# Low parts of sixteen gate weight blocks, worked out two stages early and kept in DRAM

## The chip, the core and the metric

The kernel runs on one core of one Trainium2 chip. What counts is the device time of one execution in microseconds (us), here the median of three.

## The reference

The reference is two transformer parts in a row on one sequence of 256 tokens with 1024 channels, all in float32. The first has two layers, sparse and dilated attention, each with a gated feed-forward. The second is a feed-forward at half weight, a mixer of three branches with gates, and another feed-forward. Cut to what the change touches:

```python
def swiglu(h, w_up, w_down):
    a, b = jnp.split(h @ w_up, 2, axis=-1)
    return (jax.nn.silu(a) * b) @ w_down
...
x = x + 0.5 * swiglu_ffn(rms_norm(x, ffn1_norm[l]), ffn1_w_in[l], ffn1_w_out[l])
h = rms_norm(x, mix_norm[l])
q_a, k_a, v_a, q_i, k_i, w_i, u_s, q_m, gates = jnp.split(h @ w_in[l], offsets, axis=-1)
...
g = jax.nn.sigmoid(gates.reshape(b_, s_, N_BRANCHES, D_MODEL))
merged = g[:, :, 0] * o_a + g[:, :, 1] * o_b + g[:, :, 2] * o_m
x = x + merged @ w_out[l]
x = x + 0.5 * swiglu_ffn(rms_norm(x, ffn2_norm[l]), ffn2_w_in[l], ffn2_w_out[l])
```

Here `o_a` is an attention over the 64 best keys of an index score, `o_b` a state space layer (S5) with a gated output, `o_m` an attention over 256 memory tokens. `w_in` of the mixer has 4548 columns; the last 3072 are the gates.

## The kernel before

The stages run in order: nsa (sparse attention), ffn0, dil (dilated attention), ffn1, ffn1_2, mix (mixer), ffn2_2 and the final norm. "First, second and third feed-forward" below are ffn0, ffn1 and ffn1_2. Activations lie transposed, as eight tiles of 128 channels x 256 tokens.

To keep float32 precision each operand is split into a high part that the fast matmul format holds exactly and a low part, the rest. A product is three matmuls (`mm3`, L230 to L232): high by high, low by high and high by low. Activations are split once per norm (xh, xl). Weights come as 1 MB loads `raw` on SP's DMA queue (`load`, L180; four buffers) of two blocks of 1024 rows x 128 columns. `split` makes from each block a high part wh, a copy on ScalarE (L189), and a low part wl = raw - wh, a subtraction on VectorE (L190); of wh and of wl there are four buffers each. A block then feeds 24 matmuls.

A feed-forward (`ffn`) starts with a norm: squares on ScalarE, their sum sqacc on GpSimd (L295) and TensorE (L301), then rv, rr and the factor R, copied by VectorE in two halves (L332). Products with the un-normed activations run meanwhile; each product is multiplied by R afterwards (fa, fb, L408 and L410), so the first such product needs R. `between` puts work of the second part into the loop: in ffn1 the norm of the memory tokens, in ffn1_2 the memory keys (`mem_keys`) and the S5 preparation (`s5_prepare`, with a pool `s5pre` of its own): a few hundred small operations on VectorE and GpSimd (constants s5..., rotation factors CS, a block matrix Z), whose results go to DRAM (rot_scratch, bt_scratch) and are read in the mixer as CSr and BT.

A list scheduler places the instructions by a cost model of its own: it may move work of a later stage to an earlier place where dependences and buffers allow, and each engine then runs its list in that order. Buffers are shared by address: a pool opened later can take the space of one that is closed, and then waits until that is free. `ffn1` holds a pool `hid` for its 22 pairs of hidden tiles. In the mixer, `gate(j)` makes the gates in column order; those with j > 1 are the branches S5 and memory (lists G1 and G2), sixteen blocks.

Of the kernel before, what the change touches and what calls it, by code (L numbers as in the profile page):

```python
# [11 lines left out]
F32 = mybir.dt.float32  # L12
F32R = mybir.dt.float32r
AF = mybir.ActivationFunctionType
ALU = mybir.AluOpType
# [3 lines left out]
P = 128  # L19
S = 256  # L20
D = 1024
KD = D // P
FF = 2816
# [99 lines left out]
class Builder:  # L123
# [84 lines left out]
    def ahead(self, units):  # L208

        first = next(units)  # L210
        return itertools.chain([first], units)

    def wide_units(self, w, K, c0, cols):

        res = []
        n = 1024 // cols
        for k0 in range(0, K // P, 2 * n):
            kb = min(2 * n, K // P - k0)
            v = self.load(w, k0 * P, kb, c0, cols)
            for k in range(0, kb, n):  # L220
                m = min(n, kb - k)
                res += self.split(v[:, k:k + m, :], m, cols)
        return res
# [161 lines left out]
        return X, R  # L385


    def ffn(self, xs, gain, w_up, w_down, factor, between=None, after=None, skew=0):
        nc, tc = self.nc, self.tc
        with tc.tile_pool(name=self.n("hid"), bufs=1) as hp:  # L390
            if skew:
                self.pad(hp, skew)
            if after:
                X, R = self.norm_twice(hp, xs, after, gain)
            else:
                (X,), R, _ = self.norm_all(xs, [gain])
            H = []
            for mp in range(KF // 2):
                if mp == 2 and between:
                    between()  # L400
                ua = self.units(w_up, D, mp * 256)
                ub = self.units(w_up, D, FF + mp * 256)
                for c in range(2):
                    k = 2 * mp + c
                    pa = self.proj(next(ua), X)
                    pb = self.proj(next(ub), X)
                    a = hp.tile([P, S], F32, tag="fa", name=self.n("fa"), bufs=2)
                    nc.vector.tensor_tensor(a, pa, R, ALU.mult)  # L408
                    b = hp.tile([P, S], F32, tag="fb", name=self.n("fb"), bufs=2)
                    nc.vector.tensor_tensor(b, pb, R, ALU.mult)  # L410
                    nc.scalar.activation(a, a, AF.Silu)
                    nc.vector.tensor_tensor(b, a, b, ALU.mult)
                    h = hp.tile([P, S], F32R, name=self.n("hh"), tag=f"hh{k}")
                    l = hp.tile([P, S], F32R, name=self.n("hl"), tag=f"hl{k}")
                    nc.scalar.activation(h, b, AF.Copy)
                    nc.vector.tensor_tensor(l, b, h.bitcast(F32), ALU.subtract)
                    H.append((h, l))
            self.out_proj(xs, w_down, FF, H, factor)

    def out_proj(self, xs, w, K, X, factor):  # L420
        nc = self.nc
        for mp in range(4):
            for c, u in enumerate(self.units(w, K, mp * 256)):
                ps = self.proj(u, X)
                m = 2 * mp + c
                nc.vector.scalar_tensor_tensor(xs[m], ps, float(factor), xs[m], ALU.mult, ALU.add)
# [66 lines left out]
    def key_parts(self, pool, ps, R, dst):  # L493
# [5 lines left out]
        for gp in range(2):  # L499
            h, o = slice(64 * gp, 64 * gp + 64), slice(64 - 64 * gp, 128 - 64 * gp)  # L500
            H, L = dst(gp)
            nc.scalar.activation(H[h], t[h], AF.Copy)
            nc.vector.tensor_tensor(L[h], t[h], H[h].bitcast(F32), ALU.subtract)
            nc.scalar.activation(H[o], t[h], AF.Copy)
# [616 lines left out]
    def mixer(self, xs):  # L1121
        nc, tc, A = self.nc, self.tc, self.A
        V, G = nc.vector, nc.gpsimd
        w = A["w_in_2"]
        (X,), R, _ = self.norm_all(xs, ["mix_norm_2"])
        with ExitStack() as es:
            mp = es.enter_context(tc.tile_pool(name="mix", bufs=1))
# [66 lines left out]

            def gate(j):
                for c in range(2 * j, 2 * j + 2):
                    for u in self.units(w, D, 1476 + c * 256):
                        gt = mp.tile([P, S], F32, name=self.n("sg"), tag="sg", bufs=24)
                        V.tensor_tensor(gt, self.proj(u, X), R, ALU.mult)
                        nc.scalar.activation(gt, gt, AF.Tanh, scale=0.5)  # L1200
                        yield gt
# [6 lines left out]
            for p in range(2):  # L1208
# [22 lines left out]
                for kb in range(2):  # L1231
                    for i, pt in enumerate(pts):
                        h = 2 * p + i
# [84 lines left out]
def body(tc, A, out, stages=None):  # L1318
    stages = stages or STAGES
    with ExitStack() as ctx:  # L1320
        b = Builder(ctx, tc, A)
        nc = b.nc
        xs, first = [], []
# [7 lines left out]
        if "nsa" not in stages:  # L1331
            b.bias_rows()
        late = None
        for s in stages:
            if s in ("ffn1", "fin1", "ffn1_2", "mix") and late is None:
                late = ctx.enter_context(tc.tile_pool(name="late", bufs=1))
            if s == "nsa":
                b.nsa(xs, first)
            elif s == "ffn0":
                b.ffn(xs, "norm_ffn0", A["ffn_w_up0"], A["ffn_w_down0"], 1.0)  # L1340
            elif s == "dil":
                b.dilated(xs)
            elif s == "ffn1":
                b.ffn(xs, "norm_ffn1", A["ffn_w_up1"], A["ffn_w_down1"], 1.0, lambda: b.mem_norm(late), skew=352)
                b.mem_project(late)
            elif s == "fin1" and "ffn1_2" not in stages:
                b.final(xs, "final_norm")
# [98 lines left out]
```

## Time and profile before

| | us |
|---|---|
| median of three executions | 1339.74 |
| the three | 1345.21, 1339.74, 1337.02 |
| the profiled execution | 1342.72 |
| its span | 1340.9 |
| TensorE busy | 1316.3 |
| VectorE busy | 1001.4 |
| ScalarE busy | 748.1 |
| GpSimd busy | 193.3 |

The profiled execution is a single one with a profile; its span is the time from its first to its last instruction. Its granted TensorE clock was 0.988 on average. A matmul is shown longer than the distance to the next (a pipeline), so a stretch in which TensorE is idle, or in which its clock is under 1.00, tells more than its busy time. PE, DVE, ACT, POOL and SP in rows are TensorE, VectorE, ScalarE, GpSimd and SyncE.

### The profile page before, as it was taken

To read this page: it belongs to the slowest core of one execution; us is meant where nothing else is said; L and a number is where in the kernel's file an instruction comes from. 1 tells how busy PE (TensorE), PEld (TensorE's weight loads), DVE (VectorE), ACT (ScalarE), POOL (GpSimd) and SP (SyncE) were. 2 spreads that over 40 slices of the span, in tenths; PEclk is the share of its full clock that TensorE was granted. 3 is DMA by queue.
4 is the path that set the end of the run, shared out by engine and by line. 5 is a ranking of instruction groups with operands and counts; after the bars stand their busy time and mean duration, and the time that the engine had idled before them with its cause. 6 is when DMAs were issued, how large, how long until landed. Compare 5 with 4: busy or idle time off the path is not lost.

```text
span 1340.9 us, 27511 instructions
## 1 busy us (share of the span) xinstructions
PE 1316.3 (98%) x10944; PEld 1250.6 (93%) x10944; DVE 1001.4 (75%) x2108; ACT 748.1 (56%) x1414; POOL 193.3 (14%) x236
## 2 busy tenths in 40 slices
PE   8999999999999999999999999999999999999997
PEld 8887899999999887899999999999987879999997
DVE  7899677766797663999965877766689887777743
ACT  5678555555668776654544555544434665555442
POOL 3300100001310000433100310001032044100011
PEclk8999999999999999989999999999999999999999
DMA  9742266646766340466656465655754254566561
GB/s 290 240 157 78 81 206 198 199 152 201 240 214 184 105 142 9 142 197 220 220 185 210 153 208 191 197 194 174 251 165 137 79 186 151 177 198 199 163 197 49
DMA packets 227120, 232.77 MB, mean 174 GB/s; under 512 B 5944, under 2 KB 221184, under 8 KB 226992
## 3 DMA queue, kind: packets, MB, share of 16 engines
q1 hardware_dynamic: 223392, 226.14, 53.2%
q10 hardware_dynamic: 3600, 4.88, 1.1%
q8 instruction: 86, 1.41, 0.4%
q14 instruction: 42, 0.34, 0.1%
HBM read 226.69 MB, written 4.30 MB: 172 GB/s over the span
## 4 chain that ended last, share of the span: by engine, by line
PE 56%; DVE 4%; issue 1%; ACT 1%; DMA 1%; POOL 1%; DVEq 0%; POOLq 0%; ACTq 0%
PE mm L230 7%; PE mm L231 7%; PE mm L232 7%; PE tr L232 4%; PE tr L230 4%; PE tr L231 4%; PE sc L230 4%; PE sc L231 4%; PE sc L232 4%; PE ov L230 2%; PE ov L231 2%; PE ov L232 2%; PE ov L488 1%; DVE wl L190 1%; PE sc L792 1%
## 5 line engine op out<-in xcount | busy, mean ns | idle before, releaser
L189 ACT ACTIVATE wh<-raw 128x1024 fp32r<-128x1024 f32 (+2 forms) x405 | 419.0, 1039 | 437.8 <-PE mm L231 135.4
L190 DVE TENSOR_TENSOR wl<-raw,wh 128x1024 fp32r<-128x1024 f32 (+2 forms) x405 | 490.9, 1214 | 162.6 <-ACT wh L189 157.1
L230 PE MATMUL mm<-xh,wh 128*128 128x256 f32 x952 | 272.9, 287 | 1.4 <-ACT wh L189 1.4
L231 PE MATMUL mm<-xl,wh 128*128 128x256 f32 x952 | 269.4, 283 | 0.0
L232 PE MATMUL mm<-xh,wl 128*128 128x256 f32 x952 | 269.0, 283 | 0.2 <-DVE wl L190 0.2
L230 PEld LDWEIGHTS mm<-xh,wh 128*128 128x128 f32 x952 | 181.8, 191 | 7.8 <-issue 4.7
L231 PEld LDWEIGHTS mm<-xl,wh 128*128 128x128 f32 x952 | 182.0, 191 | 3.9 <-issue 3.7
L232 PEld LDWEIGHTS mm<-xh,wl 128*128 128x128 f32 x952 | 181.3, 190 | 2.4 <-issue 1.5
L295 POOL TENSOR_TENSOR sqacc<-sqacc,sq 128x256 f32<-128x256 f32 x60 | 64.0, 1068 | 597.0 <-ACT sq L294 326.4
L230 PE MATMUL sc<-xh,wh 128*128 128x256 f32 x464 | 128.5, 277 | 0.0
L232 PE MATMUL sc<-xh,wl 128*128 128x256 f32 x464 | 128.5, 277 | 0.0
L231 PE MATMUL sc<-xl,wh 128*128 128x256 f32 x464 | 128.3, 277 | 0.0
L230 PE MATMUL tr<-xh,wh 128*128 128x256 f32 x440 | 123.4, 280 | 0.8 <-DVE u L446 0.8
L231 PE MATMUL tr<-xl,wh 128*128 128x256 f32 x440 | 123.2, 280 | 0.0
L232 PE MATMUL tr<-xh,wl 128*128 128x256 f32 x440 | 123.0, 280 | 0.0
L231 PEld LDWEIGHTS sc<-xl,wh 128*128 128x128 f32 x464 | 87.2, 188 | 0.0
L230 PEld LDWEIGHTS sc<-xh,wh 128*128 128x128 f32 x464 | 87.2, 188 | 0.0
L232 PEld LDWEIGHTS sc<-xh,wl 128*128 128x128 f32 x464 | 87.1, 188 | 0.0
L230 PEld LDWEIGHTS tr<-xh,wh 128*128 128x128 f32 x440 | 83.9, 191 | 1.1 <-DVE u L446 1.1
L231 PEld LDWEIGHTS tr<-xl,wh 128*128 128x128 f32 x440 | 84.1, 191 | 0.0
L232 PEld LDWEIGHTS tr<-xh,wl 128*128 128x128 f32 x440 | 84.0, 191 | 0.0
L230 PE MATMUL ov<-xh,wh 128*128 128x256 f32 x224 | 62.2, 278 | 0.0
(475 smaller groups left out, 3396.0 us busy)
## 6 DMA issues: line engine op xcount, KB each, us to landing
raw<-in_ffn_w_up_dram SPq DMA_DIRECT2D x44, 1024.0 KB, 5.4
raw<-in_ffn_w_in_dram SPq DMA_DIRECT2D x44, 1024.0 KB, 5.3
raw<-in_w_in_dram SPq DMA_DIRECT2D x17, 1024.0 KB, 5.3
raw<-in_ffn_w_down_dram SPq DMA_DIRECT2D x16, 1024.0 KB, 5.3
raw<-in_ffn_w_out_dram SPq DMA_DIRECT2D x16, 1024.0 KB, 5.2
raw<-in_b_w_q_dram SPq DMA_DIRECT2D x12, 1024.0 KB, 5.2
raw<-in_a_w_in_dram SPq DMA_DIRECT2D x8, 1024.0 KB, 9.2
bt<-u_scratch SPq DMA_DIRECT2D x28, 256.0 KB, 4.3
```

The lines of the kernel that those rows point to most:

```text
L189: nc.scalar.activation(hv, v, AF.Copy)
L190: nc.vector.tensor_tensor(lv, v, hv.bitcast(F32), ALU.subtract)
L230: nc.tensor.matmul(ps, sh, mh, start=(i == 0), stop=False)
L231: nc.tensor.matmul(ps, sh, ml, start=False, stop=False)
L232: nc.tensor.matmul(ps, sl, mh, start=False, stop=(i == n - 1))
L295: nc.gpsimd.tensor_tensor(acc[:, 0], acc[:, 0], s, ALU.add)
L488: nc.tensor.matmul(O[64 * i:64 * i + 64, q0:q1], V[kb], pt[:, c0:c0 + q1 - q0], start=(start and kb == 0), stop=(stop and kb == 1), skip_g ...
L792: nc.tensor.matmul(ps, Q[d, h][:, qb * P:qb * P + P], K[d][g], start=(i == 0), stop=(i == 1))
```

## The change

Sixteen blocks of the mixer's `w_in`, those of the gates with j > 1, get their low parts in ffn0 and ffn1. `low_parts` is a generator; each step loads one block (512 KB, lraw) on SP's queue, copies the high part (lh) on ScalarE, subtracts on VectorE (ll) and stores the result on ScalarE's DMA queue to a DRAM tensor low_scratch. `ffn` takes a step in every odd round of its up-projection and `out_proj` one in each of its four rounds: nine in ffn0, seven in ffn1. Its tiles (two lraw, one lh, two ll, 4 KB per partition each, 20 KB in all) lie in the pool `hid` of the feed-forward. In the mixer `low_units` replaces `units` for these blocks: raw is loaded and wh copied as before, and wl is loaded from low_scratch on SP's queue in place of the subtraction.

```diff
+    def low_parts(self, pool, w, c0, n):
+        nc = self.nc
+        self.low = nc.dram_tensor("low_scratch", (n, P, 1024), F32, kind="Internal").ap()
+        for i in range(n):
+            p = pool()
+            v = p.tile([P, 8, P], F32, tag="lraw", name=self.n("lraw"), bufs=2)
+            nc.sync.dma_start(v, w[0:D, c0 + i * P:c0 + i * P + P].rearrange("(k p) c -> p k c", p=P))
+            h = p.tile([P, 8, P], F32R, tag="lh", name=self.n("lh"), bufs=1)
+            l = p.tile([P, 8, P], F32R, tag="ll", name=self.n("ll"), bufs=2)
+            nc.scalar.activation(h, v, AF.Copy)
+            nc.vector.tensor_tensor(l, v, h.bitcast(F32), ALU.subtract)
+            nc.scalar.dma_start(self.low[i], l.bitcast(F32).rearrange("p k c -> p (k c)"))
+            yield
+
+    def low_units(self, w, c0, first):
+        nc = self.nc
+        v = self.load(w, 0, 8, c0, 256)
+        for i in range(2):
+            h = self.wsp.tile([P, 1024], F32R, tag="wh", name=self.n("wh")).rearrange("p (k c) -> p k c", c=P)
+            l = self.wsp.tile([P, 1024], F32R, tag="wl", name=self.n("wl"))
+            nc.scalar.activation(h, v[:, :, i * P:i * P + P], AF.Copy)
+            nc.sync.dma_start(l.bitcast(F32), self.low[first + i])
+            l = l.rearrange("p (k c) -> p k c", c=P)
+            yield [(h[:, k], l[:, k]) for k in range(8)]
...
+            self.low_pool = hp
             for mp in range(KF // 2):
                 if mp == 2 and between:
                     between()
+                if mp % 2 and low:
+                    next(low, None)
...
+    def out_proj(self, xs, w, K, X, factor, low=None):
         nc = self.nc
         for mp in range(4):
+            if low:
+                next(low, None)
...
-                    for u in self.units(w, D, 1476 + c * 256):
+                    for u in (self.low_units(w, 1476 + c * 256, 2 * c - 8) if j > 1 else self.units(w, D, 1476 + c * 256)):
...
+        low = b.low_parts(lambda: b.low_pool, A["w_in_2"], 2500, 16)
...
-                b.ffn(xs, "norm_ffn0", A["ffn_w_up0"], A["ffn_w_down0"], 1.0)
+                b.ffn(xs, "norm_ffn0", A["ffn_w_up0"], A["ffn_w_down0"], 1.0, low=low)
...
-                b.ffn(xs, "norm_ffn1", A["ffn_w_up1"], A["ffn_w_down1"], 1.0, lambda: b.mem_norm(late), skew=352)
+                b.ffn(xs, "norm_ffn1", A["ffn_w_up1"], A["ffn_w_down1"], 1.0, lambda: b.mem_norm(late), skew=352, low=low)
```

The change moves instructions far from its own lines. VectorE at the start of ffn1, before, where od and ol are the last tiles of the dilated attention, x the activations as its output is added, and ex, ek, eb, ep and the names with s5 belong to the S5 preparation:

```order
L266 TENSOR_TENSOR ol_6976<-od_6973,oh_6975 128x256
L871 TENSOR_SCALAR ex_10187<-vec 128x8
L915 TENSOR_TENSOR s5den<-vec 128x8
L916 TENSOR_TENSOR s5q<-vec 128x8
L872 TENSOR_SCALAR ek_10188<-ex_10187 128x8
L917 TENSOR_TENSOR s5den<-s5den,s5q 128x8
L873 TENSOR_SCALAR ek_10188<-ek_10188 128x8
L918 RECIPROCAL s5den<-s5den 128x8
L874 SCALAR_TENSOR_TENSOR ex_10187<-ek_10188,ex_10187 128x8
L876 TENSOR_SCALAR eb_10190<-ek_10188 128x8
L875 SCALAR_TENSOR_TENSOR ex_10187<-ek_10188,ex_10187 128x8
L877 TENSOR_SCALAR ep_10189<-ex_10187 128x8
```

The same place now, where xl is the low part of the norm's input, and ll a new low part:

```order
L293 TENSOR_TENSOR ol_7039<-od_7036,oh_7038 128x256
L458 SCALAR_TENSOR_TENSOR x_132<-sc_7049,x_132 128x256
L458 SCALAR_TENSOR_TENSOR x_134<-tr_7079,x_134 128x256
L985 TENSOR_SCALAR s5zc<-vec 64x8x16 x2
...
L190 TENSOR_TENSOR wl_7170<-raw_7167,wh_7169 128x1024
L190 TENSOR_TENSOR wl_7200<-raw_7167,wh_7199 128x1024
L306 SCALAR_TENSOR_TENSOR xl_7301<-x_132,gains,xh_7300 128x256
L190 TENSOR_TENSOR wl_7232<-raw_7229,wh_7231 128x1024
L190 TENSOR_TENSOR wl_7262<-raw_7229,wh_7261 128x1024
L306 SCALAR_TENSOR_TENSOR xl_7305<-x_134,gains,xh_7304 128x256
L224 TENSOR_TENSOR ll_7514<-lraw_7511,lh_7513 128x1024
```

The S5 operations are gone from here but for s5zc, and of the new low parts five stand ahead of the second copy of R, two behind it.

VectorE at the start of ffn1_2, before, around the norm's rv; mk and MV are memory keys and values:

```order
L190 TENSOR_TENSOR wl_9895<-raw_9892,wh_9894 128x1024
L190 TENSOR_TENSOR wl_9934<-raw_9861,wh_9933 128x1024
L1075 TENSOR_SCALAR MV<-sc_9704,rr_7668 128x256
L190 TENSOR_TENSOR wl_9963<-raw_9892,wh_9962 128x1024
L375 COPY ss_9820<-ov_9811 128x2
L309 TENSOR_SCALAR rv_9822<-ov_9811 128x1
```

And now:

```order
L190 TENSOR_TENSOR wl_10075<-raw_10004,wh_10074 128x1024
L905 TENSOR_SCALAR ek_10319<-ek_10319 128x8
L937 SCALAR_TENSOR_TENSOR s5th<-s5n,s5th 128x8
L906 SCALAR_TENSOR_TENSOR ex_10318<-ek_10319,ex_10318 128x8
L908 TENSOR_SCALAR eb_10321<-ek_10319 128x8
L937 SCALAR_TENSOR_TENSOR s5th<-s5n,s5th 128x8
L907 SCALAR_TENSOR_TENSOR ex_10318<-ek_10319,ex_10318 128x8
L937 SCALAR_TENSOR_TENSOR s5th<-s5n,s5th 128x8
L402 COPY ss_9932<-ov_9923 128x2
L336 TENSOR_SCALAR rv_9934<-ov_9923 128x1
```

The S5 preparation, which stood at the start of ffn1, now begins behind the last addition to x of ffn1; 36 of its operations on VectorE stand ahead of the first rv and 28 more ahead of the second copy of R. On GpSimd its memsets of Z and CS now stand between the third and the fourth of this norm's twelve sums.

SP's queue in the mixer's gates, before:

```order
L180 DMA raw_13528<-in_w_in_dram 128x8x256
L1021 DMA CSr_13048<-rot_scratch 128x512
L1011 DMA BT_13099<-bt_scratch 128x2x512
L180 DMA raw_13594<-in_w_in_dram 128x8x256
L1021 DMA CSr_13066<-rot_scratch 128x512
L180 DMA raw_13660<-in_w_in_dram 128x8x256
```

And now:

```order
L180 DMA raw_13640<-in_w_in_dram 128x8x256
L236 DMA wl_13445<-low_scratch 128x1024
L1053 DMA CSr_13160<-rot_scratch 128x512
L236 DMA wl_13477<-low_scratch 128x1024
L180 DMA raw_13706<-in_w_in_dram 128x8x256
L1043 DMA BT_13211<-bt_scratch 128x2x512
L1053 DMA CSr_13178<-rot_scratch 128x512
L236 DMA wl_13511<-low_scratch 128x1024
L1053 DMA CSr_13214<-rot_scratch 128x512
L236 DMA wl_13543<-low_scratch 128x1024
L180 DMA raw_13772<-in_w_in_dram 128x8x256
```

The sixteen low loads stand in line with raw and CSr loads; six CSr loads lie between the first and the last of them. On TensorE the index scores and the first head scores of the mixer stand about 40 rows later than before.

## Rows read from the trace of the kernel before

**Rows 1.** The page's head: span; then busy us, share and instructions of each engine.

```profile
span 1340.9 us, 27511 instructions
...
PE 1316.3 (98%) x10944; PEld 1250.6 (93%) x10944; DVE 1001.4 (75%) x2108; ACT 748.1 (56%) x1414; POOL 193.3 (14%) x236
```

**Rows 2.** The page's groups: high and low parts (busy, mean ns; idle before, releaser).

```profile
L189 ACT ACTIVATE wh<-raw 128x1024 fp32r<-128x1024 f32 (+2 forms) x405 | 419.0, 1039 | 437.8 <-PE mm L231 135.4
L190 DVE TENSOR_TENSOR wl<-raw,wh 128x1024 fp32r<-128x1024 f32 (+2 forms) x405 | 490.9, 1214 | 162.6 <-ACT wh L189 157.1
```

**Rows 3.** Stretches of 33.5 us: busy us of each engine, granted clock, DMA share, GB/s.

```profile
134.00:167.50 33.50, 33.40 (x275) 29.91 (x270) 22.13 (x39) 17.90 (x34) 6.18 (x9) 1.00 0.25 79
536.00:569.50 33.50, 30.56 (x241) 29.77 (x242) 31.60 (x100) 22.16 (x40) 14.25 (x18) 0.95 0.45 142
569.50:603.00 33.50, 31.37 (x248) 31.18 (x247) 31.10 (x96) 19.48 (x33) 12.07 (x14) 0.90 0.61 197
603.00:636.50 33.50, 33.50 (x298) 33.50 (x297) 32.79 (x96) 17.07 (x25) 11.82 (x17) 1.00 0.68 220
737.00:770.50 33.50, 33.35 (x281) 33.27 (x280) 26.93 (x48) 18.10 (x31) 12.87 (x14) 0.95 0.48 152
971.00:1004.50 33.50, 33.45 (x255) 30.03 (x254) 28.94 (x55) 12.18 (x20) 12.09 (x10) 1.00 0.53 165
1072.00:1105.50 33.50, 32.25 (x233) 26.68 (x233) 27.51 (x82) 22.48 (x63) 14.09 (x14) 1.00 0.60 189
1105.50:1139.00 33.50, 31.89 (x266) 31.10 (x265) 26.74 (x43) 17.34 (x27) 16.00 (x20) 1.00 0.44 143
```

**Rows 4.** The same, stretches of 5 us.

```profile
538.00:543.00 5.00, 3.21 (x18) 3.01 (x19) 4.94 (x9) 3.56 (x9) 2.70 (x2) 0.80 0.09 15
578.00:583.00 5.00, 4.52 (x21) 4.52 (x22) 4.97 (x16) 2.48 (x5) 0.81 (x3) 0.55 0.09 14
983.00:988.00 5.00, 5.00 (x34) 4.17 (x33) 4.99 (x11) 1.18 (x4) 2.12 (x2) 1.00 0.41 124
```

**Rows 5.** Timeline of TensorE, 535 to 579: start, us; idle before and releaser.

```profile
540.12 0.38 PE L232 MATMUL sc<-oh,wl 128*128 128x256 f32 x1 [1.79 <-DVE wl L190]
...
578.48 0.56 PE L301 MATMUL ov<-ones,sqacc 128*128 128x1 f32 x2 [2.13 <-POOL sqacc L295]
```

**Rows 6.** Timeline of VectorE, 533 to 534.

```profile
533.09 0.17 DVE L871 TENSOR_SCALAR ex<-vec 128x8 f32<-128x8 f32 x1
...
533.33 1.02 DVE L872 TENSOR_SCALAR ek<-ex 128x8 f32<-128x8 f32 x1
```

**Rows 7.** Timeline of GpSimd, 534 to 755.

```profile
534.97 1.18 POOL L958 MEMSET Z<- 128x1280 f32 x1
...
576.27 2.16 POOL L295 TENSOR_TENSOR sqacc<-sqacc,sq 128x256 f32<-128x256 f32 x1 [4.22 <-DVE cl L1001]
...
742.58 3.14 POOL L295 TENSOR_TENSOR sqacc<-sqacc,sq 128x256 f32<-128x256 f32 x3 [1.25 <-ACT sqacc L289]
...
748.22 6.66 POOL L295 TENSOR_TENSOR sqacc<-sqacc,sq 128x256 f32<-128x256 f32 x5 [0.43 <-ACT sq L294]
```

**Rows 8.** Timeline of VectorE, 756 to 770.

```profile
756.09 0.21 DVE L309 TENSOR_SCALAR rv<-ov 128x1 f32<-128x1 f32 x2
...
768.25 0.28 DVE L332 COPY R<-ov 128x128 f32<-128x128 f32 x1
...
769.76 0.42 DVE L408 TENSOR_TENSOR fa<-tr,R 128x256 f32<-128x256 f32 x1
```

**Rows 9.** DMA issues: count, KB each, median us to landing.

```profile
raw<-in_w_in_dram SPq DMA_DIRECT2D x17, 1024.0 KB, 5.3
...
raw<-in_w_in_dram SPq DMA_DIRECT2D x2, 512.0 KB, 4.1
```

**Rows 10.** What SP's queue waited for, 938 to 1140: us, times, longest.

```profile
SPq L180 <- DVE wl L190: 76.4, 16, 7.4
SPq L1021 <- DVE xn L1036: 21.3, 5, 5.8
```

More of the change, by code (lines that the diff above doesn't have):

```diff
@@ L385, in norm_twice, with ffn @@
         return X, R
-    def ffn(self, xs, gain, w_up, w_down, factor, between=None, after=None, skew=0):
+    def ffn(self, xs, gain, w_up, w_down, factor, between=None, after=None, skew=0, low=None):
         nc, tc = self.nc, self.tc
@@ L417, in ffn @@
                     H.append((h, l))
-            self.out_proj(xs, w_down, FF, H, factor)
-    def out_proj(self, xs, w, K, X, factor):
+            self.out_proj(xs, w_down, FF, H, factor, low)
+    def out_proj(self, xs, w, K, X, factor, low=None):
         nc = self.nc
         for mp in range(4):
+            if low:
+                next(low, None)
             for c, u in enumerate(self.units(w, K, mp * 256)):
```

## The prediction

> **What bounds the kernel now.** I read the page's head first: TensorE is busy for 1316.3 of 1340.9 us, VectorE for 1001.4, ScalarE for 748.1 [rows 1]. The reader sees that TensorE sets the time nearly everywhere, and that a change of VectorE's work is worth something only where TensorE stands still for it. So the second view is the table by stretch of 33.5 us [rows 3]. Two things count there: how much of 33.5 TensorE is idle, and how far its granted clock is under 1.00. At the start of the first feed-forward (134 to 167.5) it loses 0.1 us. At the start of the second (536 to 603) it loses 2.94 and 2.13 us by idling, and a mean clock of 0.95 and 0.90 takes 1.7 and 3.35 us more: 10.1 us in all. At the start of the third (737 to 770.5) it loses 0.15 and 1.7 us. The gates of the mixer (971 to 1004.5) lose 0.05 us, the end of the mixer (1072 to 1139) 1.25 and 1.61 us. The finer table [rows 4] shows VectorE full in two places with opposite results: 4.94 of 5 us at 538 with TensorE at 3.21, and 4.99 of 5 at 983 with TensorE at 5.00. A full VectorE alone isn't a loss; it is one where TensorE needs the next thing from it. The 33.5 us from 603 say the same: VectorE 32.79, TensorE 33.50 [rows 3].
>
> The timelines name the thing at 536. TensorE waits 1.79 us for a low part behind a run of small S5 operations on VectorE, and 2.13 us at 578 for the sum of squares [rows 5]. That addition on GpSimd took 2.16 us, after GpSimd had stood idle 4.22 us for an S5 operation of VectorE [rows 7]. TensorE's clock lies at half (1.2 of 2.4 GHz) for part of the stretch right behind each gap: means of 0.80 and 0.55 [rows 4].
>
> **The profiled execution.** It took 1342.72 us (span 1340.9), 3 us over the median of 1339.74. The sum below is a difference, and I put it on the median.
>
> **What is removed and added.** A low part costs VectorE 1.214 us and its high part ScalarE 1.039 us [rows 2]. The mixer loses 16 subtractions: 19.4 us of VectorE. In exchange nine blocks of low parts go to the first feed-forward (10.9 us of VectorE, 9.4 of ScalarE) and seven to the second (8.5 and 7.3), each with a 512 KB load on SP's queue and a 512 KB store on ScalarE's. The mixer gains 16 loads of 512 KB on SP's queue; its own raw loads and high parts stay. I take each term by its place.
>
> **Mixer, the gates.** VectorE is full here and gets 19.4 us of room, but TensorE loses 0.05 us in 33.5 [rows 3], so the room buys nothing directly. What it costs is transfers: 8.4 MB over about 100 us is 84 GB/s on top of 165, and the DMA share would rise from 0.53 [rows 3] to about 0.8 (an estimate, in proportion). A 512 KB load lands in 4.1 us, a 1 MB one in 5.3 [rows 9]. The order shows each low load some 10 us of TensorE work ahead of its use, since only the four low buffers hold it back; 4.1 us fit twice. The risk is SP's order: six loads of rotation factors (CSr) now stand between low loads, and SP waits for such a load's buffer up to 5.8 us [rows 10]. Behind a waiting one all later low loads and raw loads are queued, and then TensorE. Price: 0 to +5.8.
>
> **Mixer, the end.** If VectorE arrives earlier at the top-k and the heads, the idle 1.25 and 1.61 us [rows 3] can go; the order puts the index scores and heads on TensorE about 40 rows later, which is as likely to take it back. Price: -2.9 to 0. For the whole mixer I take +0.5, nearest to nothing, since neither the wait nor the gain is in a row of this place.
>
> **First feed-forward.** Eight of nine low parts stand in the norm and the first groups, five ahead of the second copy of R, which every gated product needs. Five are 6.1 us of VectorE. VectorE has 11.4 us to spare in the 33.5 there, ScalarE 15.6 [rows 3], and part of that lies ahead of R. Cost: 0 to +3 (half of the 6.1), I take +1.
>
> **Second feed-forward.** This is the largest term, and no line of the diff names it. The low tiles add 20 KB per partition to the pool of the feed-forward, and by the order the S5 preparation no longer starts beside it: of its operations only those on s5zc and the memsets of KM and s5zc stay. The run of small operations ahead of the additions to x is gone, and GpSimd's sums have no S5 product among them. So both named waits (1.79 and 2.13) lose their cause, and with them the half clock that follows (1.7 and 3.35): 9.0 of the 10.1 us. Against it stand five low parts ahead of R, 6.1 us of VectorE and 5.2 of ScalarE, where VectorE had 1.9 us spare in 33.5 with S5's work and has more without it [rows 3]. The memory norm's sum stands 71 rows later on TensorE, some 8 us more time for it (at one row in 33.5/298 us). Bounds: -10.1 (all goes) to 0 (the low parts take S5's place). I take -7.5, near to the end for which the waits have names.
>
> **Third feed-forward.** The S5 preparation goes here. Some 36 small operations now stand on VectorE ahead of the norm's rv and 28 more ahead of the second copy of R; small ones start 0.08 us apart where nothing holds them (three steps from 533.09 to 533.33, [rows 6]), so 2.9 and 2.2 us. On GpSimd the 1.18 us memset of Z and two of CS come between the sums [rows 7]. R is copied at 768.25 and first used at 769.76 [rows 8]: 1.5 us to spare. So R would come 0 to 6.3 us late, TensorE wait 0 to 4.8, and a gap that long brings a stretch of half clock like those above (1.7 to 3.35): 0 to +8.2, with a little for the low rest +9. VectorE has 6.6 us spare in these 33.5 [rows 3] and many of the small operations fall there, so I take +3.5. What is left of the preparation runs later beside plain products, as in 603 to 636.5, where a VectorE at 98% cost nothing.
>
> The trace shows more than length, though. One S5 operation took 1.02 us where its like took 0.17, beside memsets of GpSimd [rows 6], and one addition on GpSimd took 2.16 us where three took 3.14 together [rows 7]. The Trainium skill, SBUF — State Buffer, section "SBUF: two separate sides", says that VectorE and GpSimd share one pair of ports, which whoever starts first holds for its whole instruction while the other is blocked. The trace agrees in kind, by the 2.16 against 1.05. By that rule moving S5's work beside the third feed-forward's sums is worse than my sum: the second rival, below, would hold, and the sum would be its sum.
>
> **Sum.** -7.5 + 3.5 + 1 + 0.5 = -2.5 us: 1339.74 - 2.5 = **1337**. With every term at its low end -13.0, at its high end +17.8.
>
> **The rivals.**
> 1. The mixer is bound by VectorE. For it: 4.99 of 5 us [rows 4], and SP waits 76.4 us in sixteen times for low parts of VectorE [rows 10]. Then the 19.4 us come off the path: 1339.74 - 19.4 = 1320. Against it: TensorE has no idle time there for them to come out of.
> 2. Whatever fills VectorE ahead of R delays TensorE. The low parts keep the 10.1 us at the second feed-forward as they are (term 0), and at the third the twelve sums of squares take 2.16 us each in place of 1.05, 13.3 us, less the 1.5 to spare, with 3.35 of half clock: +15.2. With +1.5 from the other terms 1339.74 + 16.7 = 1356. It decides as soon as R is later than its 1.5 us of cover. For it: that is what [rows 5, 7] show of the second feed-forward. Against it: the sums overlap transfers and copies of ScalarE, and S5's dense part comes only after R in the new order.
> 3. The low loads come late. SP's five waits of 21.3 us [rows 10] then fall on loads that gates need; each has about 5 us of cover, so some 8 us are left: 1337 + 8 = 1345.
> 4. The change does nothing: every moved instruction has cover on both sides, and the waits at 536 come from something else: 1340.
>
> **How the numbers follow.** About 1%, 13 us, is what a measurement of this kernel can tell from no change. The forecast has 0.50, with its own range of 1331 to 1344; rival 4 0.14; rival 3 0.12; rival 2 0.12; rival 1 0.12. Faster by over 1% (under 1326) is rival 1 with a sliver of the forecast: 0.13. Slower by over 1% (over 1353) is rival 2 with a part of rival 3: 0.14. The rest, 0.73, is within 1%. The range holds the forecast, rivals 3 and 4 and the near ends of the others: from 1325 (all terms at their low end, 1326.7, and a little) to 1352 (+12, two thirds of the high sum).
>
> **What would show it.** Right, if the new trace has no S5 operation at the second feed-forward's start, TensorE's waits for the low part and the sum of squares are gone there, and its clock is 1.00; if R at the third feed-forward comes 2 to 5 us later after the last addition to x, with a gap on TensorE of 1 to 4 us; and if the gates show VectorE with some 19 us less and TensorE as full as before. Wrong, if the gates get shorter (rival 1), if the additions at the third feed-forward take 2 us each (rival 2), or if TensorE waits for a DMA of a low part (rival 3). The sum also rests on the order alone for where the S5 preparation goes; if it starts at another time than that shows, the two largest terms fall together.

## The result, and the profile after

The changed kernel is slower: 1349.33 us against 1341.84 (medians of nine each), a ratio of 1.0067, 95% interval 1.0051 to 1.0083, or some 9 us (7 to 11). It lies within the range that was given (1325 to 1352), on the other side of no change from the forecast of 1337. The profiled execution took 1349.33 us, the median itself.

The page's head, as in [rows 1]:

```profile
span 1347.2 us, 27644 instructions
...
PE 1316.7 (98%) x10944; PEld 1248.1 (93%) x10944; DVE 998.0 (74%) x2108; ACT 757.9 (56%) x1429; POOL 190.7 (14%) x236
```

TensorE's busy time is the same within 0.4 us; its idle time grew. The stretches of [rows 3], with the same columns:

```profile
134.00:167.50 33.50, 31.75 (x243) 28.08 (x241) 21.94 (x34) 19.25 (x34) 7.72 (x8) 0.95 0.52 158
536.00:569.50 33.50, 29.92 (x246) 28.69 (x245) 29.41 (x44) 24.10 (x39) 11.48 (x12) 1.00 0.92 287
569.50:603.00 33.50, 31.69 (x262) 31.29 (x261) 26.53 (x44) 21.39 (x35) 6.40 (x6) 0.95 0.84 279
...
737.00:770.50 33.50, 31.67 (x237) 31.47 (x236) 29.08 (x104) 16.69 (x30) 12.22 (x20) 0.85 0.44 141
971.00:1004.50 33.50, 33.50 (x263) 30.47 (x261) 19.59 (x44) 11.98 (x18) 9.84 (x8) 1.00 0.82 270
1072.00:1105.50 33.50, 32.16 (x227) 27.30 (x226) 30.67 (x98) 18.95 (x49) 12.28 (x13) 1.00 0.61 188
```

A row gives the stretch and its length, then the busy time of TensorE, its weight loads, VectorE, ScalarE and GpSimd, then TensorE's granted clock, the DMA engines' busy share and GB/s. Read line by line: the first feed-forward's start loses 1.75 us by idling and 1.7 by the clock, where it lost 0.1. The second's loses 3.6 and 1.8 by idling and 1.7 by the clock: 7.1 in place of 10.1, so the gain is less than half of what was forecast. The third's loses 1.8 and 5.0 in place of 1.85. The gates gave up 9 us of VectorE in these 33.5 (28.94 to 19.59) and TensorE is as full as it was.

Where TensorE stood still, from its timeline:

```profile
150.81 0.39 PE L257 MATMUL ov<-oh,wh 128*128 128x256 f32 x1 [0.77 <-ACT wh L189]
151.75 0.39 PE L257 MATMUL mm<-oh,wh 128*128 128x256 f32 x1 [0.45 <-ACT wh L189]
152.70 0.39 PE L257 MATMUL sc<-oh,wh 128*128 128x256 f32 x1 [0.44 <-ACT wh L189]
...
540.95 0.38 PE L259 MATMUL sc<-oh,wl 128*128 128x256 f32 x1 [1.43 <-DVE wl L190]
...
554.89 0.38 PE L258 MATMUL tr<-xl,wh 128*128 128x256 f32 x1 [0.95 <-DVE xl L306]
...
578.68 0.39 PE L257 MATMUL mm<-xh,wh 128*128 128x256 f32 x1 [1.05 <-ACT wh L189]
579.94 0.39 PE L259 MATMUL mm<-xh,wl 128*128 128x256 f32 x1 [0.76 <-DVE wl L190]
...
753.70 0.39 PE L259 MATMUL tr<-xh,wl 128*128 128x256 f32 x1 [1.83 <-DVE wl L190]
```

The wait for the sum of squares [rows 5] is gone from the second feed-forward. The other named wait, for a low part of the weights, is still there: 1.43 us at 541, where it was 1.79, although only the six operations on s5zc are left of S5 there. New are waits for xl, wh and wl at 555 and 579, where VectorE and ScalarE have low parts among them.

Three timelines say why. ScalarE at the first feed-forward:

```profile
148.75 1.06 ACT L223 ACTIVATE lh<-lraw 128x1024 fp32r<-128x1024 f32 x1 [3.74 <-DMA lraw<-in_w_in_dram]
149.72 1.98 ACT L189 ACTIVATE wh<-raw 128x1024 fp32r<-128x1024 f32 x2
```

The first low block's copy stands ahead of the first weights' copies; TensorE's waits from 150.81 on are for such copies. Before, with the first addition to x at 149.6, they came at once:

```profile
149.53 2.97 ACT L189 ACTIVATE wh<-raw 128x1024 fp32r<-128x1024 f32 x3 [3.03 <-PE tr L231]
```

Now that addition starts at 148.15 and the first of them at 149.72, some 1.7 us later than it would by the same distance: 0.7 us in which ScalarE waits for the low block's load, and 1.0 us of its copy. The load was issued late, as SP's queue shows:

```profile
144.71 6.75 SPq L220 DMA_DIRECT2D lraw<-in_w_in_dram  x3
```

VectorE at the third feed-forward, between 748 and 754:

```profile
748.87 0.70 DVE L911 SCALAR_TENSOR_TENSOR ep<-ep,ex 128x8 f32<-128x8 f32 x1
749.49 1.92 DVE L306 SCALAR_TENSOR_TENSOR xl<-x,gg,xh 128x256 fp32r<-128x256 f32 x2
...
752.43 1.21 DVE L190 TENSOR_TENSOR wl<-raw,wh 128x1024 fp32r<-128x1024 f32 x1
```

S5 operations, some stretched, push the norm's xl and then a low part of the weights back, and TensorE waits 1.83 us for that one, at 753.70. The runs bear this out: the same wait of 1.83 us, as far behind the last addition to x, stands in the profiles of e1 and e2, which have S5 in this place too, and in none of those that have it elsewhere. Its clock in the 5 us stretches behind:

```profile
752.00:757.00 5.00, 3.30 (x19) 3.31 (x19) 4.93 (x14) 1.20 (x2) 0.01 (x1) 0.75 0.00 0
757.00:762.00 5.00, 5.00 (x25) 5.00 (x25) 4.38 (x35) 0.83 (x2) 1.64 (x4) 0.50 0.79 252
762.00:767.00 5.00, 5.00 (x34) 5.00 (x34) 2.81 (x20) 1.60 (x3) 0.86 (x3) 0.73 0.53 171
```

The mean is 0.75, 0.50 and 0.73, so 5.1 us are lost at 1.2 GHz behind a gap of 1.83. In the mixer, TensorE's waits have a new line:

```profile
PE mm L259 <- DMA wl<-low_scratch: 0.4, 1, 0.4
```

### The profile page after: what moved, and what is told of

It is laid out like the page before. It is cut to its first block, busy times and chain, and to the rows that moved or that the text cites. A ratio compares the mean times of both kernels' runs of the same rounds, so it can differ in the third digit from the quotient of the medians.

```text
span 1347.2 us, 27644 instructions
## 1 busy us (share of the span) xinstructions
PE 1316.7 (98%) x10944; PEld 1248.1 (93%) x10944; DVE 998.0 (74%) x2108; ACT 757.9 (56%) x1429; POOL 190.7 (14%) x236
## 4 chain that ended last, share of the span: by engine, by line
PE 52%; DVE 7%; DMA 3%; issue 1%; ACT 1%; POOL 1%; SPq 0%; DVEq 0%; ACTq 0%; POOLq 0%
PE mm L257 6%; PE mm L259 6%; PE mm L258 6%; PE tr L259 4%; PE tr L257 4%; PE tr L258 4%; PE sc L258 3%; PE sc L257 3%; PE sc L259 3%; DVE wl L190 2%; PE ov L257 2%; PE ov L258 2%; PE ov L259 2%; PE ov L520 1%; DMA lraw<-in_w_in_dram 1%
## 5 line engine op out<-in xcount | busy, mean ns | idle before, releaser
L189 ACT ACTIVATE wh<-raw 128x1024 fp32r<-128x1024 f32 (+2 forms) x389 | 400.7, 1035 | 364.7 <-PE mm L258 95.5
L190 DVE TENSOR_TENSOR wl<-raw,wh 128x1024 fp32r<-128x1024 f32 (+2 forms) x389 | 470.3, 1212 | 153.6 <-ACT wh L189 148.6
L257 PE MATMUL mm<-xh,wh 128*128 128x256 f32 x952 | 269.9, 284 | 2.8 <-ACT wh L189 2.8
```

Of the source, the lines that this page charges most:

```text
L189: nc.scalar.activation(hv, v, AF.Copy)
L190: nc.vector.tensor_tensor(lv, v, hv.bitcast(F32), ALU.subtract)
L257: nc.tensor.matmul(ps, sh, mh, start=(i == 0), stop=False)
```

## The experiments

For every kernel the time between additions to x is taken from its profile: the first feed-forward (from the first addition before it to its last), the second, the third (from the last addition of the second to its own last) and the mixer (on to its last). The ratio is of timed runs (six for e2 and five for e3, eight to twelve for the others).

| kernel | first | second | third | mixer | ratio to before, 95% |
|---|---|---|---|---|---|
| before | 194.4 | 204.9 | 199.3 | 208.2 | 1 |
| changed | 198.1 | 203.8 | 205.1 | 209.7 | 1.0067 [1.0051, 1.0083] |
| e1_gap_only | 194.7 | 200.3 | 202.6 | 208.3 | 1.0013 [0.9998, 1.0028] |
| e2_low_unused | 198.5 | 203.8 | 203.0 | 208.4 | 1.0074 [1.0049, 1.0098] |
| e3_mixer_only | 197.9 | 209.1 | 198.3 | 210.0 | 1.0053 [1.0038, 1.0068] |
| e4_all_in_first | 205.4 | 204.3 | 197.7 | 210.5 | 1.0046 [1.0028, 1.0064] |
| e5_low_in_ring | 194.3 | 206.8 | 197.6 | 210.3 | 1.0026 [1.0011, 1.0041] |
| e6_ring_unused | 194.4 | 206.3 | 198.4 | 208.1 | 1.0010 [0.9997, 1.0022] |
| e7_mixer_ring | 194.4 | 201.0 | 197.7 | 210.1 | 1.0011 [0.9997, 1.0025] |
| e8_s5_later | 194.4 | 208.4 | 195.9 | 207.7 | 1.0041 [1.0025, 1.0056] |
| e9_s5_slack2 | 194.4 | 201.7 | 197.5 | 208.1 | 0.9995 [0.9984, 1.0006] |
| e10_s5_slack3 | 194.3 | 206.6 | 198.9 | 208.4 | 0.9989 [0.9973, 1.0005] |
| e11_after_s5_slack3 | 201.5 | 202.8 | 200.5 | 213.4 | 1.0061 [1.0037, 1.0085] |
| e12_ring_s5_slack3 | 194.3 | 199.0 | 199.1 | 209.5 | 0.9985 [0.9963, 1.0007] |
| e13_ring_first | 194.4 | 204.1 | 199.6 | 210.4 | 1.0010 [0.9992, 1.0027] |
| e14_low_on_gpsimd | 197.1 | 205.0 | 198.1 | 209.8 | 1.0030 [1.0011, 1.0049] |

The columns are single executions. The first is steady (194.3 to 194.7 wherever no low part has tiles of its own) and so is the mixer (207.7 to 208.4 without low loads). The second isn't: kernels with the same S5 place and no low part in it (before, e3, e4, e7, e13, e14) span 201.0 to 209.1. So differences there are read from timed runs, not from one profile.

Part of this scatter is TensorE's own pace, with no wait and no half clock. The same 33.5 us away from any start, TensorE busy throughout, for the second feed-forward in e3 and in e7:

```profile
640.00:673.50 33.50, 33.50 (x286) 33.50 (x286) 30.77 (x53) 17.26 (x26) 5.77 (x4) 1.00 0.67 220
...
640.00:673.50 33.50, 33.50 (x298) 33.50 (x298) 29.27 (x45) 18.16 (x28) 1.04 (x1) 1.00 0.74 237
```

That is 4% fewer matmuls at a granted clock of 1.00, some 7 us over a feed-forward. So it is in e10's second, in a part of e6's second and in e4's first (287 in 200 to 233.5), not in the first, second and third feed-forward of before, changed and e1. No run shows what sets it.

**e1_gap_only**, the memory alone (both pools):

```diff
+            if gap:
+                t = hp.tile([P, gap // 4], F32, name=self.n("gap"))
+                nc.gpsimd.memset(t[:, :8], 0.0)
...
```

> The kernel before with 20 KB per partition left empty in the pools of the first and second feed-forward; no low parts, mixer as before. The order shows the S5 preparation at the start of the third feed-forward, as in the changed kernel. Theory S (the place of the S5 preparation): the third feed-forward loses the 5.9 us that the changed kernel lost there, with a TensorE gap near 1.8 us and a clock at half for some 10 us; the second, with nothing in S5's place, gains 6 to 9 us: 1 to 3 us faster in all. Rival L (low parts): what the changed kernel lost came from the low parts; the S5 preparation is hidden in the third feed-forward too, so 5 us or more faster. Rival N: the losses at the start of the second feed-forward were never S5's: no gain there, 5 to 6 us slower.

Measured: 1.7 us slower (-0.3 to +3.8), not told apart from no change. None of the three expectations came in its numbers. The S5 preparation alone, moved by 20 KB, costs about what it gains:

```profile
536.00:569.50 33.50, 32.63 (x264) 32.23 (x265) 28.32 (x45) 24.10 (x45) 13.82 (x14) 0.95 0.56 181
569.50:603.00 33.50, 32.15 (x282) 31.95 (x281) 26.48 (x46) 18.59 (x31) 2.04 (x2) 1.00 0.61 196
737.00:770.50 33.50, 31.67 (x277) 31.47 (x276) 32.98 (x130) 17.25 (x32) 12.22 (x18) 1.00 0.44 141
```

The second feed-forward's start loses 0.9, 1.35 and 1.7 us, 3.9 in place of 10.1 (4.6 in stretches moved to where this stage starts here, 2.1 us earlier); the third's idles 1.8. What TensorE waits for at the second has changed: 0.3 us are left of the wait for the low part, and 1.4 us for rr of GpSimd, a step of a norm, are new. Theory S, by which the place of S5 explains the changed kernel's loss, falls.

**e2_low_unused**, the mixer as before:

```diff
-                    for u in (self.low_units(w, 1476 + c * 256, 2 * c - 8) if j > 1 else self.units(w, D, 1476 + c * 256)):
+                    for u in self.units(w, D, 1476 + c * 256):
```

> The changed kernel with the mixer of before: the low parts are worked out and stored, and nothing reads them. Theory S: the mixer's share of the loss is small (1.5 us by the two traces), so 5 to 7 us slower than before. If the mixer's loads are the real cost (rival M): within 2 us of before.

Measured: 9.9 us slower (6.6 to 13.1). The loss of the changed kernel is all there without its mixer. Against e1, which has the same memory and the same S5 place, some 8 us are the low parts (6 by the two medians; e2 has six executions, one of them at 1359).

**e3_mixer_only**, one low part in tiles of its own (the order has it at the first feed-forward's start, though it is written in the eighth round):

```diff
-            nc.sync.dma_start(l.bitcast(F32), self.low[first + i])
+            nc.sync.dma_start(l.bitcast(F32), self.low[0])
...
-                if mp % 2 and low:
+                if mp == 7 and low:
...
-        low = b.low_parts(lambda: b.low_pool, A["w_in_2"], 2500, 16)
+        low = b.low_parts(lambda: b.low_pool, A["w_in_2"], 2500, 1)
...
```

> Only the mixer's half: one low part is worked out in the first feed-forward, none in the second, and all sixteen loads of the mixer read this one block (the output is not the reference's). The order shows the S5 preparation at the start of the second feed-forward, as before. Theory S: 0 to +2 us in the mixer, with VectorE some 19 us less busy there; up to +2 at the first feed-forward if a single high copy ahead of ScalarE's queue is enough for its gap. In all 0 to +4. Rival M (late low loads): +5 or more in the mixer. Rival V (the mixer is bound by VectorE): 5 us or more faster.

Measured: 7.1 us slower, more than either the theory or the profile's 3.5 at the first feed-forward and 1.8 in the mixer explains; the second feed-forward was long in that one profile, by TensorE's slower pace (above). TensorE's gaps at the first are those of the changed kernel (0.64, 0.45 and 0.45 us for wh), from a single low part.

**e4_all_in_first**, all sixteen in the first feed-forward (a step in every round, five in the down-projection, none in the second):

> All sixteen low parts in the first feed-forward, none in the second; mixer as in the changed kernel. The order shows the S5 preparation at the start of the second feed-forward, as before. Theory S: the third feed-forward is as before, the second as before, the first loses 2 to 5 us, the mixer 1 to 2: 3 to 6 us slower. Rival L (low parts cost by their number): the first feed-forward loses 5 us or more.

Measured: 6.2 us slower. The third feed-forward, with S5 back at its old place, is as short as any. The first lost 11.0 in the profiled execution (1352.48 us, above the median of 1347.68), which by its number is Rival L. But its waits are those of the changed kernel (0.88, 0.45 and 0.45 us for wh), idle time and half clock take 3.9 there, and the other 7 are TensorE's slower pace (above). So nothing shows that the number counts: one, nine and sixteen blocks (e3, changed, e4) lose 3.5 to 4 by waits and clock. By time, sixteen in the first (3.8 to 8.6) can't be told apart from nine there and seven in the second (7 to 11).

**e5_low_in_ring**, the low part made in the weights' own buffers:

```diff
-            v = p.tile([P, 8, P], F32, tag="lraw", name=self.n("lraw"), bufs=2)
...
+            v = self.load(w, 0, 8, c0 + i * P, P)
+            h = self.wsp.tile([P, 1024], F32R, tag="wh", name=self.n("wh"))
+            l = self.wsp.tile([P, 1024], F32R, tag="wl", name=self.n("wl"))
...
```

> The changed kernel, but a low part is made with the buffers of the weights themselves (raw, wh, wl) instead of tiles of its own: it then stands in its turn between the blocks of the feed-forward, behind the second copy of R, and takes no memory, so the S5 preparation stays at the start of the second feed-forward. Theory P (position: the low parts cost where the scheduler put them, ahead of the high copies that TensorE's first blocks need): the feed-forwards lose 0 to 1 us, the mixer keeps the 1.5 us of its loads: 0 to 3 us slower than before. Rival N (number: sixteen subtractions, copies, loads and stores cost wherever they stand): 6 to 10 us slower, as the changed kernel.

Measured: 3.5 us slower (1.5 to 5.5). Same sixteen copies, subtractions, loads and stores as in the changed kernel, 5.5 us less. Theory P holds, though its numbers ended at 3. Here S5 is also back at its old place; e12 against e11 has it in one place.

**e6_ring_unused**, the same with the mixer of before:

> The same low parts in the buffers of the weights, and the mixer of before, which reads none of them. Theory P: within 1.5 us of before, where the unused low parts of the changed kernel's form cost 10 us. Rival N: 6 to 10 us slower. If the mixer's loads cost anything, this one is faster than the run with low parts in the ring that the mixer reads, by 1 to 2 us.

Measured: 1.3 us slower (-0.4 to 3.0) where the same unused low parts in tiles of their own cost 9.9. The difference to e5, 2.2 us, is the mixer's loads, with an interval of some 2 us on each of the two.

**e7_mixer_ring**, e3 with its one low part in the weights' buffers:

> The mixer's half as in the run with one low part, but this one low part is made in the buffers of the weights in the eighth round of the first feed-forward (all sixteen loads read it; the output is not the reference's). Theory P: the first feed-forward is as before, the mixer costs 0 to 2 us, 0 to 2 slower, so that 4 to 5 of the 7 us of the earlier run were the one low part at the feed-forward's start. Rival M (the mixer's loads are the cost): 5 to 7 us slower, no better than the earlier run.

Measured: 1.5 us slower (-0.4 to 3.4), against 7.1: one load, one copy, one subtraction and one store at another place in the queues, with S5 in the same place, are worth 5.6 us, of which the first feed-forward shows 3.5. The tiles' memory isn't it: with that alone (e1) the first is at 194.7.

**e8_s5_later**, S5 held by a zero from a hidden tile:

```diff
+            V.tensor_scalar(z, hold[:, 0:1].bitcast(F32), 0.0, None, ALU.mult)
+            V.tensor_scalar(ld, self.v("log_dt", 8), z, None, ALU.add)
...
+                if mp == 2 and middle:
+                    middle(h)
...
```

> No low parts, mixer as before; only the S5 preparation is held until the third round of the second feed-forward (a zero taken from a hidden tile is added to its first input), behind both copies of R. If its operations at the start of that feed-forward cost what the profile of before shows there (two waits and the half clock behind them), it is 3 to 8 us faster than before, and the S5 operations vanish in rounds in which VectorE is 75% busy. If those losses were never S5's: within 1.5 us of before.

Measured: 5.5 us slower, against the expectation. What TensorE waited for between 585 and 745 (us in total, times, longest):

```profile
PE ov L979 <- DVE CS L1000: 2.7, 1, 2.7
PE ov L230 <- ACT bt L981: 2.0, 1, 2.0
PE ov L979 <- DVE Z L975: 0.2, 1, 0.2
```

The preparation has a step on TensorE (Z turned, L979), and the order had put it ahead of products that were ready.

**e9_s5_slack2**, the same written behind the eighth round (`if mp == 7`, with the tile of the third):

> No low parts. The S5 preparation in the second feed-forward again, held until its third round, but written behind the eighth round, so that its TensorE and ScalarE steps stand later in their queues. In the earlier run of this kind the start gained some 6 us in its profile and a wait of TensorE for Z and bt (4.9 us, with half clock behind it) took them back. Theory: without that wait the gain stays, 3 to 6 us faster than before. Rival: the S5 operations cost TensorE about as much wherever they stand, within 1.5 us of before or slower.

Measured: even with before, 0.7 us faster (-2.1 to +0.8). The waits at L979 are gone, one of 1.1 us for bt stays. The rival holds by its number.

**e10_s5_slack3**, held in the third feed-forward instead:

> No low parts. The S5 preparation is held until the third round of the third feed-forward and written behind its eighth. With only the empty 20 KB it stood at that stage's start and was about even with before (+1.8 us): by the profiles 4 to 6 us gained at the second feed-forward's start, 3 to 4 lost at the third's. Theory: what was lost at the third was its place ahead of the first blocks; held, the loss goes and the gain stays: 3 to 6 us faster than before. Rival: the loss comes with the operations, wherever: within 2 us of before.

Measured: 1.5 us faster (-3.6 to +0.7), not told apart from no change. Between the two, by its number.

**e11_after_s5_slack3**, the changed kernel with that hold:

> The changed kernel with the S5 preparation held in the same way in the third feed-forward. Theory: of its 9 us the 4 to 6 of the third feed-forward go, those of the low parts at the starts of the first and the second (7 us by the profiles, against the one with the empty 20 KB) stay: 3 to 6 us slower than before. Rival L (all of it is the low parts): 7 us or more slower.

Measured: 8.2 us slower (5.0 to 11.4): Rival L by its number, though the interval reaches into the theory's 3 to 6. Taking S5 out of the third feed-forward's start gives the changed kernel nothing that the timing can tell, though its third stage is 4.6 us shorter in the profile. That execution had a longer mixer, with the largest wait for a low load of all:

```profile
PE mm L259 <- DMA wl<-low_scratch: 2.1, 1, 2.1
```

**e12_ring_s5_slack3**, low parts in the weights' buffers and S5 held:

> Low parts made in the buffers of the weights, read by the mixer, and the S5 preparation held in the third feed-forward. Theory: the sum of the two runs, that is the run without low parts and with the S5 preparation held, plus the 2 to 4 us that the low parts in the ring and the mixer's loads cost: within 2 us of before, and slower than that run by 2 to 4. Rival V (the mixer gains once its loads meet no other cost): as fast as that run or faster.

Measured: 2.0 us faster (-5.0 to +0.9), not told apart from no change, nor from e10; the sum of e5 and e10, +2.0, is just outside its interval, but each of those has one of some 2 us of its own. The mixer is again 1.3 us longer in the profile, so Rival V has no support there; the 2 to 4 us over e10 that were expected did not show either. Against e11 it is the cleanest pair: the same sixteen blocks, the same loads in the mixer and S5 in the same place, and 10 us less (1337.60 against 1347.18 by the medians) for low parts in the weights' buffers. No version beats the kernel before clear of the noise.

**e13_ring_first**, e7 with its step ahead of the norm:

> One low part in the buffers of the weights, as in the run with the mixer's half, but as the first block of the first feed-forward, ahead of its weights; its load is issued with the weights of the stage before, since its buffer is one of the four raw ones. All sixteen loads of the mixer read it (the output is not the reference's). If standing ahead of the first weights is what costs (a copy of 1 us on ScalarE and a subtraction of 1.2 us on VectorE first): the first feed-forward loses 2 to 4 us, 4 to 6 slower than before in all. If ScalarE's wait for the late load is what costs: 0 to 1 us there, and 1 to 3 slower than before, as the run with this block in the eighth round.

Measured: 1.3 us slower, the first feed-forward at 194.4. It does not decide what it was made for: ScalarE made this block's copy at 155.29, behind the first four weights' copies. It shows once more that a low part behind these costs that stage nothing.

**e14_low_on_gpsimd**, e3 with copy, subtraction and store on GpSimd:

```diff
+            nc.gpsimd.tensor_copy(h, v)
+            nc.gpsimd.tensor_tensor(l, v, h.bitcast(F32), ALU.subtract)
+            nc.gpsimd.dma_start(self.low[i], l.bitcast(F32).rearrange("p k c -> p (k c)"))
...
```

> The run with one low part in tiles of its own, whose load comes late, but copy, subtraction and store are GpSimd's (the output is not the reference's, as there). ScalarE and VectorE then have nothing of it in their queues. If ScalarE's in-order wait carried the loss: TensorE has no gap at the first high copies of the first feed-forward, the stage loses under 1.5 us by its profile, 1 to 3 slower than before in all. If SP's queue or the transfer carried it: the gap of 1.5 us and the half clock behind it stay, 5 to 7 slower.

Measured: 4.0 us slower (1.5 to 6.6), 3 less than e3, and between the two expectations. ScalarE's copies come at once (147.18, where the load lands at 147.9) and TensorE's waits for wh are gone. But the first feed-forward still loses 2.7 us, where under 1.5 was expected. GpSimd's subtraction took 3.25 us, VectorE's two next to it were slow, and TensorE has new waits for wl, xl and xh, 1.5 us together. GpSimd and VectorE here, then VectorE in e3:

```profile
149.04 3.25 POOL L224 TENSOR_TENSOR ll<-lraw,lh 128x1024 fp32r<-128x1024 f32 x1
...
150.29 4.76 DVE L190 TENSOR_TENSOR wl<-raw,wh 128x1024 fp32r<-128x1024 f32 x2
...
152.90 2.35 DVE L190 TENSOR_TENSOR wl<-raw,wh 128x1024 fp32r<-128x1024 f32 x2
```

So the low block's place in ScalarE's queue, its wait and its copy together, carried the gap for wh, but the run can't say what would remain with neither.

## Why the prediction was wrong

What bounds the kernel was right: the gates' 19.4 us of VectorE bought nothing, and the mixer term (+0.5) was small and of the right sign. It measured +1.3 to +2.3 in eight of nine profiles with low loads (+5.2 in e11) and 2.2 by e5 against e6. Rival 3's mechanism is there at a small scale, a wait of 0.3 to 2.1 us for a low load; its 8 us did not follow from its own rows, since five waits of 21.3 us, none over 5.8, with 5 us of cover each leave under 3. Rival 1 is out.

**The step that failed is the low parts' cost at the starts, and with it the gain from moving S5.** The first feed-forward was put at +1, from the room that VectorE and ScalarE have over 33.5 us. It cost +3.7, above its upper bound of 3, and one low part costs as much as nine (e3, +3.5; e11, again with nine, lost 7.1 in its profile, with a further wait of 1.9 us for wh). Room over a stretch says nothing on the 5 us in which TensorE changes over to new weights. There the copy of a low block stood ahead of the weights' copies, and waited itself. Its load was issued only at 144.71. The gaps sum to 1.66 us, the half clock behind them takes 1.7.

**The second feed-forward** was put at -7.5 with a bound of 0 "if the low parts take S5's place". That bound was the case, for the greater part: the profile shows -1.1, and -4.6 with the same memory and no low parts (e1). That "both named waits lose their cause" was half true. The wait for the sum of squares did go; that for the low part stayed at 1.43 us, and without low parts it was 0.3 to 1.2 (e1, e8 to e10), so S5 was not its only cause. Waits for xl, wh and wl came on top, with transfers at 0.92 and 0.84 of the engines' time. As the second column scatters, the timed pairs carry this: e2 against e1, some 8 us for low parts at both starts.

**The third** was put at +3.5 for a late R, and cost +5.8. Place and direction were right, the carrier was wrong. R did come 5.1 us later (27.4 us behind the last addition to x in place of 22.3), but TensorE did not wait for it. It waited for a weight's low part, 15 us ahead of R, and the half clock behind that cost 3.3 us more than before. With the same wait and no half clock behind it the stage cost +3.3 in e1 and +3.7 in e2: so near to the forecast by luck, since another wait carried it. The twelve sums were no slower, as GpSimd's timeline shows beside [rows 7]:

```profile
742.21 3.27 POOL L322 TENSOR_TENSOR sqacc<-sqacc,sq 128x256 f32<-128x256 f32 x3
...
747.84 4.17 POOL L322 TENSOR_TENSOR sqacc<-sqacc,sq 128x256 f32<-128x256 f32 x5 [0.53 <-ACT sq L321]
```

So the second rival's price was wrong: what the prediction feared from the Trainium skill (SBUF — State Buffer, section "SBUF: two separate sides") did not show at this place. Its sentence "whatever fills VectorE ahead of R delays TensorE" came nearest of all, and it had a chance of 0.12.

**S5 moved alone** was worth -4 in the sum (-7.5 and +3.5) and measured +1.7 (e1, -0.3 to +3.8); held clear of both starts, -1.5 to -0.7 (e9, e10). So of the 10.1 us at the second feed-forward little is to be had by moving S5. The wait for the sum of squares goes with it in all three, but 0.7 to 1.4 us for rr come in its place, and 0.3 to 1.2 are left of that for the low part. What takes the rest back in the timed runs stays open; in e10's profile TensorE's slower pace takes some 7 us of the second.

The sum by places, +3.7, -1.1, +5.8 and +1.5, is 9.9, with -1.4 in the dilated attention (its first addition comes 190.9 us after the feed-forward, before 192.3), which nobody had counted: 8.5, against 9 timed. That -1.4 goes with S5: with it in the third feed-forward (e1, e2, e10 to e12) the figure is 190.9 to 191.1, with it in the second 192.3 to 192.9. The two profiled spans differ by 6.3 only, because the profile of before is long elsewhere: 1.5 us ahead of the first feed-forward and 0.7 in the last.

## What to carry to other kernels

Work that was moved to where an engine has room on average was free here only where it stood behind what the next stage waits for; under a scheduler that places by data and buffers, a tile of its own was ready early and went to the front (e3). Putting it through the ring of buffers that the stage's own work uses keeps it in its turn, here 5.5 us for the same sixteen blocks (e5 against changed), 10 with S5 in one place (e12 against e11). A profile of one execution can differ by some 7 us in a stage that the edit leaves as it was (e3's second). And 20 KB of tiles can move a stage that no line of the diff names: compare the orders first, then time the memory alone.

## What the hardware showed unasked

Behind a gap of 1.83 us on TensorE, at the third feed-forward, the clock lay at half for so long that the 15 us from 752 have a mean of 0.66 (0.75, 0.50, 0.73). One of 1.43 us in the same execution, at 541, was followed by none (1.00 over 536 to 569.5, above, and in the 5 us around it):

```profile
538.00:543.00 5.00, 3.06 (x21) 2.65 (x22) 4.89 (x11) 5.00 (x9) 0.65 (x1) 1.00 0.76 202
```

In the kernel before, 1.79 us at the same place had a mean of 0.80 in the 5 us around it [rows 4]. And the gap of 1.83 us itself, at the same place in e1, had a clock of 1.00 behind it:

```profile
750.00:755.00 5.00, 5.00 (x45) 5.00 (x45) 4.97 (x36) 1.49 (x4) 1.50 (x4) 1.00 0.64 206
```

What decides stays open. And beside a GpSimd subtraction of two SBUF tiles (3.25 us) and the additions behind it, two VectorE subtractions took 4.76 us in place of 2.35 (e14 against e3). The same section of the Trainium skill describes that, an exclusive hold of a shared pair of ports, for a VectorE instruction with two inputs in SBUF against a GpSimd one that reads SBUF. Here the trace agrees, by the 4.76 against 2.35.
